# Attention probabilities split into f16 pairs in rows and transposed by DMA, value products one step later, norms summed along rows

## The chip, the cores and the metric

The kernel runs on one core of a Trainium2 chip. The metric is the device time of one execution in microseconds (us). A core has TensorE (PE in the profile; its weight loads are PEld), VectorE (DVE), ScalarE (ACT), GpSimd (POOL) and SyncE (SP). Here SP does no arithmetic: it issues every DMA of the kernel, in one queue, in order.

## The reference, cut to what matters

One layer over 2048 tokens of width 1024, all in float32. Only the parts that the change meets are quoted in full:

```
h = rms_norm(x, g1)                        # mean of x*x over a token's 1024 values
p = h @ W_in                               # q, k, v of 8 heads x 64, conv and pool channels
q = rms_norm(q);  k = rms_norm(k)          # per head
scores = q k^T / 8 + bias(head, distance)  # own 64-token chunk and the 8 chunks before it
probs  = softmax(scores);  y = probs @ v
x = x + concat(y, conv, pool) @ W_out
x = x + square(relu(rms_norm(x, g2) @ W1)) @ W2      # 1024 -> 4096 -> 1024
```

## The kernel before

The work is done in four blocks of 512 tokens (`block`, L385) and then in an MLP stage (L995) that needs all blocks. A float32 product is made from pairs (a high part, and what is left of it), with three matmuls for a product (`mm3`, L159). In the MLP, and for probabilities times values, both parts are f16.

**A block.** `project` (L402) is called three times, for q, k and v. In the first call `load_x` (L390) also loads x transposed (features on partitions), splits it, squares it (ACT, L208) and adds the squares up on POOL (L209); four small TensorE products with a column of ones (`token_cols`, L211, L214) sum this over the features, and `rsqrt` turns it into a factor for each token. Then attention runs, woven with dense work.

**Attention** has 32 units in a block: 4 head pairs x 2 heads x 4 tiles of 128 query rows. A unit has up to 5 tiles of 128 keys (640 columns; in block 0 only 1 to 4 tiles, since nothing lies before it). `scores` (L517) makes the scores on TensorE (L529, L530), adds the bias and takes the row maximum on DVE (L533), and takes the exponential on ACT (L539) into `sb`: 128 queries x up to 640 keys, float32. `flip` (L542) transposes `sb` with TensorE in tiles of 128x128 against the identity (L550), at most 512 columns into one PSUM bank `pt`; ACT makes the f16 high part from PSUM (L551), scaled by `PSC`, and DVE the rest (L552), both into `pp` (two buffers). `values` (L555) multiplies each tile of `pp` by the values, three matmuls of 64 columns for each key tile (L565).

**Order.** `weave` (L75) writes the order of TensorE's instructions by hand: for each step of `attention` (L581) it takes a share of the side work, which is the output projection of the block before, then the conv and pool channels of this one (`side`, L760). Within the step of unit n, TensorE gets the scores of n, side work, the transposes of unit n-1, the value products of unit n-2, and side work. TensorE follows that order strictly. The other engines and SP have an order of their own, fixed when the program is built, with `attention` given the higher priority; each runs it in order.

**Surveys.** The MLP works in f16 with scales taken from the norms of its weights. `survey` (L267) loads all of W1 and W2 once (128 loads of 256 KB, `pr` L281 and `ps` L298) in small steps among the side work. For W1 it squares on ACT (L283), adds three times on POOL (L286 to L288) and sums with TensorE products against ones (L271). For W2 each row's sum comes from ACT's accumulator (L300). In block 3, `early_operands` (L348) prepares the first MLP operands among the conv steps.

**Buffers.** `scr`, `hd` and `p1` lie in SBUF. A tile of a pool with `bufs=n` takes the place of the n-th one before it, and its first writer waits until all readers of that one are done, DMAs included.

Of the kernel before, what the change touches and what calls it, by code (L numbers as in the profile page):

```python
# [18 lines left out]
P = 128  # L19
# [73 lines left out]
def trunk(ctx, tc, xT, cols, cinv, w_qkv, w_cp, w_out, w1, w2, nbias, pool_w, outT):  # L93
# [32 lines left out]
    ones16 = const.tile([P, 1], BF16, name="ones16")  # L126
    ve.memset(ones16, 1.0)
# [75 lines left out]
    def sumsq(acc, src, first, pool):  # L203
        if first:
            sc.activation(acc, src, AF.Square)
        else:
            q = pool.tile([P, TB + 16], F32, tag="win", bufs=2, name="sq")[:, :TB] if pool is scr else pool.tile([P, 512], F32, tag="sq", bufs=1, name="sq")
            sc.activation(q, src, AF.Square)  # L208
            gp.tensor_tensor(out=acc, in0=acc, in1=q, op=ALU.add)  # L209
# [16 lines left out]
    vacc = p1.tile([P, 512], F32, name="vacc")  # L226
# [11 lines left out]
    def value_norms(k):  # L238
        raw = scr.tile([P, 512], F32, tag="x", bufs=5, name=f"vw{k}")
# [18 lines left out]
    cn = const.tile([P, FF // P], F32, name="cn")  # L258
# [8 lines left out]
    def survey():  # L267
        def norms(f0, group):
            t = pd(f"cn{f0}")
            for i in range(8):  # L270
                te.matmul(t[:, i : i + 1], group[:, i], ones16, start=True, stop=True)  # L271
            ve.tensor_copy(cn[:, f0 : f0 + 8], t[:, 0:8])

        full = None
        for ft in range(FF // P):
            if ft % 8 == 0:
                group = scr.tile([P, 8, P], BF16, tag="pg", bufs=2, name=f"pg{ft}")
            qs = []
            for half in range(2):
                raw = scr.tile([P, 512], F32, tag="x", bufs=5, name=f"pr{ft}_{half}")  # L280
                sy.dma_start(raw, w1[ft, half])  # L281
                q = scr.tile([P, 4, P], BF16, tag="pq", bufs=3, name=f"pq{ft}_{half}")
                paced(sc.activation(q.rearrange("p a b -> p (a b)"), raw, AF.Square))  # L283
                qs.append(q)
            q = qs[0]
            gp.tensor_tensor(out=q, in0=q, in1=qs[1], op=ALU.add)  # L286
            gp.tensor_tensor(out=q[:, :2], in0=q[:, :2], in1=q[:, 2:], op=ALU.add)
            gp.tensor_tensor(out=group[:, ft % 8], in0=q[:, 0], in1=q[:, 1], op=ALU.add)  # L288
            if ft % 8 == 2 and full:
                norms(*full)  # L290
            if ft % 8 == 7:
                full = (ft - 7, group)
            yield
        yield
        norms(*full)
        for i in range(64):
            raw = scr.tile([P, 512], F32, tag="x", bufs=5, name=f"ps{i}")
            sy.dma_start(raw, w2[i // 16, (i // 2) % 8, i % 2])  # L298
            q = scr.tile([P, 512], BF16, tag="pq", bufs=3, name=f"pt{i}")
            paced(sc.activation(q, raw, AF.Square, accum_out=sq2[:, i : i + 1]))  # L300
            if i % 2:
                yield

# [21 lines left out]
    def scales():  # L325
        for _ in surveyed:
            pass
        m = const.tile([P, 4], F32, name="m")
        ve.tensor_reduce(out=m[:, 0:1], in_=cn, axis=AX.X, op=ALU.max)
# [12 lines left out]
        ve.tensor_scalar(m[:, 3:4], m[:, 3:4], 2.0**-17, None, op0=ALU.mult)  # L342
        ve.tensor_tensor(out=beta, in0=m[:, 3:4], in1=p[:, 1:2], op=ALU.mult)
# [4 lines left out]
    def early_operands():  # L348
        for k in range(4):
            q = {}  # L350
            for n in range(2):
                rr = scr.tile([P, 512], F32, tag="x", bufs=5, name=f"er{k}_{n}")
                sy.dma_start(rr, r2d[n])
                for half in range(2):
                    kk = k + 4 * half
                    t = scr.tile([P, 512], F32, tag="x", bufs=5, name=f"e{k}_{half}{n}")
                    sy.dma_start(t, x2d[kk, :, n * 512 : n * 512 + 512])
                    ve.scalar_tensor_tensor(out=t, in0=t, scalar=g2s[:, kk : kk + 1], in1=rr, op0=ALU.mult, op1=ALU.mult)
# [26 lines left out]
    def block(b, prev_out):  # L385
        t0 = b * TB
        xgs = [p1.tile([P, 2, TB], F32R, tag="xg", bufs=KT, name=f"xg{b}_{k}") for k in range(KT)]
        acc = p1.tile([P, TB], F32, tag="acc", name=f"acc{b}")

        def load_x(k):  # L390
            xr = scr.tile([P, 512], F32, tag="x", bufs=5, name=f"x{b}_{k}")
            sy.dma_start(xr, xT[k * P : (k + 1) * P, t0 : t0 + TB])
            g = col[:, C_G1 + k : C_G1 + k + 1]
            xg = xgs[k]
            sc.activation(xg[:, 0], xr, AF.Copy, scale=g)
            ve.scalar_tensor_tensor(out=xg[:, 1], in0=xr, scalar=g, in1=xg[:, 0].bitcast(F32), op0=ALU.mult, op1=ALU.subtract)
            sumsq(acc, xr, k == 0, scr)
# [4 lines left out]
        def project(c, also=lambda k: None):  # L402
# [3 lines left out]
            else:  # L406
                ac = [pd(f"a{b}_{c}_{i}", "dydt"[i]) for i in range(4)]
            for k in range(KT):
                if c == 0:
                    load_x(k)  # L410
                w = load_w(w_qkv[c, k], f"wq{b}_{c}_{k}", 1)
# [4 lines left out]
                also(k)  # L416
            return ac

        acq = project(0)
        ms1 = token_cols(acc, f"ms1_{b}")  # L420
        rstd = rsqrt(sm, ms1, NT, "r1")
        epsq = sm.tile([P, NT], F32, tag="epsq", name=f"epsq{b}")
        ve.tensor_scalar(epsq, ms1, EPS, None, op0=ALU.mult)
# [80 lines left out]
        ve.tensor_scalar(vr, rstd, vsc[:, 0:1], None, op0=ALU.mult)  # L504
# [7 lines left out]
        rb = row_bcast(rstd, f"rb{b}")  # L512
# [29 lines left out]
        def flip(u, st, sb, lo_t, nk, vp):  # L542
            hp, j, i = u
            h = 2 * hp + j
            pp = hd.tile([P, 2, 640], F16, tag="pp", name=f"pp{b}_{h}_{i}")
            for c0, c1 in ((0, nk),) if nk <= 512 else ((0, 384), (384, nk)):
                pt = pd(f"pt{b}_{h}_{i}_{c0}", "t")
                n = c1 - c0
                for m in range(n // P):
                    te.transpose(pt[:, m * P : (m + 1) * P], sb[:, c0 + m * P : c0 + (m + 1) * P], ident)  # L550
                sc.activation(pp[:, 0, c0:c1], pt[:, :n], AF.Copy, scale=PSC)  # L551
                ve.scalar_tensor_tensor(out=pp[:, 1, c0:c1], in0=pt[:, :n], scalar=PSC, in1=pp[:, 0, c0:c1], op0=ALU.mult, op1=ALU.subtract)  # L552
            return u, st, pp, lo_t, nk // P, vp

        def values(u, st, pp, lo_t, nkt, vp):  # L555
# [525 lines left out]
```

## Time and profile before

| what | value |
|---|---|
| median of 3 runs | 2143.21 us (2143.02 to 2146.45) |
| the profiled execution | 2144.97 us; span of its instructions 2143.1 us |
| mean granted TensorE clock | 0.986 of full speed |
| busy: PE, DVE, ACT, POOL | 96%, 64%, 47%, 33% of the span |
| DMA | 58% of the span of 16 engines, 392.88 MB |
| attention of blocks 0 to 3, first score matmul to last | about 86 to 164, 252 to 402, 489 to 637, 743 to 885 us |
| MLP stage | from about 970 us to the end |

Time outside the span is 1.9 us. "Busy" of an engine is the union of its instructions' spans. "Idle before" names what ended a wait, by the semaphores. DMA share is the mean busy share of the 16 DMA engines. "Landing" is the time from a DMA's issue to its completion.

### The profile page before, as it was taken

The numbers are of one execution on the slowest core, as the hardware profiler recorded it, in microseconds if no ns is written. First come the engines' busy times: TensorE is split into PE (matmuls) and PEld (weight loads), VectorE is DVE, ScalarE is ACT, GpSimd is POOL, SyncE is SP. The second block draws the span as 40 slices with busy tenths as digits, with TensorE's granted clock in tenths as the row PEclk, the third lists the DMA queues.
The fourth block names the chain that finished last, engine by engine and source line by source line (L and its number), as shares of the span: only waits on it lengthen the run. The fifth ranks groups of instructions, "written<-read, shape, count | busy, mean of one in ns | idle before, by whom it ended". The sixth has DMA issues, their size and how long they took to land.

```text
span 2143.1 us, 31845 instructions
## 1 busy us (share of the span) xinstructions
PE 2050.1 (96%) x11136; PEld 1262.3 (59%) x11136; DVE 1365.9 (64%) x2184; ACT 1010.9 (47%) x1940; POOL 700.1 (33%) x565
## 2 busy tenths in 40 slices
PE   7999998999899699998999999999999999999999
PEld 6777787888787588864444444444444444444444
DVE  7687466856679767757768878767743053353354
ACT  5466465737665455545656446446134151150330
POOL 4254055200224213154546456445522031130132
PEclk9999999999999899999999999999999999999999
DMA  8685698549866776493465565547743333333344
GB/s 287 202 242 169 173 273 248 179 121 273 266 199 211 241 225 179 136 344 116 161 221 189 174 209 182 182 148 286 259 120 102 104 101 101 103 97 106 103 148 152
DMA packets 215824, 392.88 MB, mean 183 GB/s; under 512 B 25584, under 2 KB 32880, under 8 KB 215664
## 3 DMA queue, kind: packets, MB, share of 16 engines
q1 hardware_dynamic: 215664, 390.86, 58.2%
q8 instruction: 87, 1.43, 0.3%
q14 instruction: 73, 0.60, 0.1%
HBM read 268.60 MB, written 105.38 MB: 175 GB/s over the span
## 4 chain that ended last, share of the span: by engine, by line
PE 68%; DMA 10%; DVE 9%; issue 5%; POOL 4%; ACT 3%; SPq 1%; POOLq 0%; DVEq 0%; ACTq 0%
PE b_d L845 21%; PE b_u L845 18%; PE a L161 3%; PE a L162 3%; PE a L160 3%; PE cp L160 2%; PE o L160 2%; PE cp L161 2%; PE cp L162 2%; PE o L161 2%; PE o L162 2%; PE pt L550 2%; PE y L565 2%; DMA r_d<-w 1%; PE s L529 1%
## 5 line engine op out<-in xcount | busy, mean ns | idle before, releaser
L845 PE MATMUL b_d<-ft_u,s_d 128*128 128x512 f16 x1152 | 265.8, 381 | 7.6 <-ACT ft_u L795 3.2
L845 PEld LDWEIGHTS <-s_d 128*128 128x128 f16 x1536 | 150.5, 98 | 191.3 <-issue 10.6
L845 PEld LDWEIGHTS <-s_u 128*128 128x128 f16 x1536 | 150.6, 98 | 186.5 <-issue 7.2
L845 PE MATMUL b_u<-zt,s_u 128*128 128x512 f16 x1152 | 257.3, 381 | 1.5 <-DVE u2u L948 0.8
L966 DVE TENSOR_TENSOR acc<-acc,b_d 128x512 f32<-128x512 f32 x176 | 119.1, 682 | 179.7 <-PE b_d L845 175.4
L845 PEld LDWEIGHTS <-a_u 128*128 128x128 f16 x1152 | 112.8, 98 | 146.6 <-issue 13.5
L845 PEld LDWEIGHTS <-a_d 128*128 128x128 f16 x1152 | 112.8, 98 | 143.2 <-issue 8.4
L829 POOL TENSOR_TENSOR t1u<-u2u,c11u 128x512 f32<-128x512 f32 x32 | 43.6, 1363 | 443.5 <-ACT u2u L952 431.3
L845 PE MATMUL b_d<-fb_u,a_d 128*128 128x512 f16 x768 | 183.7, 379 | 4.0 <-DVE acc L966 1.7
L845 PE MATMUL b_u<-zb,a_u 128*128 128x512 f16 x768 | 176.6, 379 | 1.3 <-ACT u2u L935 1.3
L209 POOL TENSOR_TENSOR acc<-acc,sq 128x512 f32<-128x512 f32 x56 | 82.8, 1479 | 260.4 <-ACT sq L208 191.3
L161 PE MATMUL a<-wq,xg 128*128 128x512 f32 x384 | 155.3, 404 | 8.2 <-DVE wq L142 8.2
L160 PE MATMUL a<-wq,xg 128*128 128x512 f32 x384 | 147.4, 407 | 10.4 <-ACT wq L141 7.8
L162 PE MATMUL a<-wq,xg 128*128 128x512 f32 x384 | 154.5, 403 | 0.1
L539 ACT ACTIVATE sb<-sb,nm 128x640 f32<-128x640 f32 (+4 forms) x128 | 97.6, 762 | 115.8 <-DVE nm L533 111.5
L552 DVE SCALAR_TENSOR_TENSOR pp<-pt,pp 128x384 f16<-128x384 f32 (+1 forms) x224 | 101.8, 483 | 48.2 <-ACT pp L551 47.6
L533 DVE CUSTOM_DVE_ANT_0 sb<-s,b 128x640 f32<-128x640 f32 (+4 forms) x128 | 94.1, 735 | 52.7 <-PE s L530 51.3
L142 DVE TENSOR_TENSOR wq<-rwq,wq 128x512 fp32r<-128x512 f32 x96 | 79.9, 839 | 46.0 <-ACT wq L141 46.0
L160 PE MATMUL o<-mix,wo 128*128 128x512 f32 x256 | 106.3, 416 | 1.3 <-ACT mix L631 1.0
L160 PE MATMUL cp<-xg,wc 128*128 128x512 f32 x256 | 107.1, 418 | 0.0
L141 POOL CAST wc<-rwc 128x512 fp32r<-128x512 f32 x64 | 41.8, 653 | 195.4 <-PE cp L162 94.2
L935 ACT COPY u2u<-b_u 128x512 f32<-128x512 f32 x32 | 18.5, 578 | 179.8 <-PE b_u L845 177.5
(274 smaller groups left out, 4512.1 us busy)
## 6 DMA issues: line engine op xcount, KB each, us to landing
rwq<-w_qkv SPq DMA_DIRECT2D x96, 256.0 KB, 2.8
pr<-w SPq DMA_DIRECT2D x64, 256.0 KB, 4.8
rwc<-w_cp SPq DMA_DIRECT2D x64, 256.0 KB, 4.3
rwo<-w_out SPq DMA_DIRECT2D x64, 256.0 KB, 4.4
ps<-w SPq DMA_DIRECT2D x64, 256.0 KB, 4.5
r_u<-w SPq DMA_DIRECT2D x64, 256.0 KB, 3.4
wd<-s_u SPq DMA_DIRECT2D x64, 256.0 KB, 2.2
r_d<-w SPq DMA_DIRECT2D x64, 256.0 KB, 2.9
```

What stands on the lines that cost most here:

```text
L142: (lo or ve).tensor_tensor(out=w[:, 1], in0=raw, in1=w[:, 0].bitcast(F32), op=ALU.subtract)
L160: te.matmul(out, ah, bh, start=start, stop=False)
L161: te.matmul(out, ah, bl, start=False, stop=False)
L162: te.matmul(out, al, bh, start=False, stop=stop)
L209: gp.tensor_tensor(out=acc, in0=acc, in1=q, op=ALU.add)
L533: ve.tensor_tensor_reduce(out=sb[:, :nk].rearrange("p (e k) -> p e k", e=ne), in0=s[:, :ne, :hk], in1=bi[:, 640 - nk :].rearrange("p (e k) ...
L539: exps.append(sc.activation(sb[:, :nk], sb[:, :nk], AF.Exp, bias=nmx, scale=-1.0, accum_out=st["l"][:, i, j : j + 1]))
L550: te.transpose(pt[:, m * P : (m + 1) * P], sb[:, c0 + m * P : c0 + (m + 1) * P], ident)
L552: ve.scalar_tensor_tensor(out=pp[:, 1, c0:c1], in0=pt[:, :n], scalar=PSC, in1=pp[:, 0, c0:c1], op0=ALU.mult, op1=ALU.subtract)
L829: gp.tensor_tensor(out=t1, in0=b12, in1=b11, op=ALU.subtract)
L845: te.matmul(bank, w[:, a, q * P : (q + 1) * P], xs[q][:, c], start=start and q == 0 and i == 0, stop=q == n - 1 and i == 2, skip_group_che ...
L966: ve.tensor_tensor(out=a, in0=a, in1=bk, op=ALU.add)
```

## The change

The scores stay as they are. `flip` no longer uses TensorE: ACT makes the f16 high part directly from `sb` in rows, DVE the rest, both into a new tile `ph` with **one** buffer, and SP issues two DMA transposes (one for each part) from `ph` to `pp`, which now has three buffers. The value products of a unit come one step later (unit n-3 in the step of unit n). Token norms of x come from a second copy of x in rows (`xN`, 32 more loads of 256 KB), squared and summed by ACT's accumulator; W1's norms in the same way from a transposed copy (`w1t`), as W2's already were. With it go the POOL sums of these norms and their TensorE products. `early_operands` loads `r2d` twice instead of eight times and loads a step ahead. Several scratch pools get other sizes.

```diff
 def survey():
+    srcs = [w1t[i // 2, i % 2] for i in range(64)] + [w2[i // 16, (i // 2) % 8, i % 2] for i in range(64)]
+    held = []
+    def look():
+        i, raw = held.pop(0)
+        acc = (sq1, sq2)[i // 64][:, i % 64 : i % 64 + 1]
+        paced(sc.activation(raw, raw, AF.Square, accum_out=acc))
+    for i, src in enumerate(srcs):
+        raw = scr.tile([P, 512], F32, tag="sv", bufs=4, name=f"{'prt'[2 * (i // 64)]}{i}")
+        sy.dma_start(raw, src)
+        held.append((i, raw))
+        if i % 2:
+            while len(held) > 2:
+                look()
+            yield
...
 def load_x(k):
-    xr = scr.tile([P, 512], F32, tag="x", bufs=5, name=f"x{b}_{k}")
+    xr = scr.tile([P, 512], F32, tag="sv", bufs=4, name=f"x{b}_{k}")
...
-    sumsq(acc, xr, k == 0, scr)
+def row_power(n):
+    raw = scr.tile([P, 512], F32, tag="sv", bufs=4, name=f"xn{b}_{n}")
+    sy.dma_start(raw, xN[4 * b + n // 2, n % 2])
+    return n, raw
+def look_rows(n, raw):
+    sc.activation(raw, raw, AF.Square, accum_out=sx[:, n // 2, n % 2 : n % 2 + 1])
...
-ms1 = token_cols(acc, f"ms1_{b}")
+    ve.tensor_reduce(out=ms1, in_=sx, axis=AX.X, op=ALU.add)
+    ve.tensor_scalar(ms1, ms1, 1.0 / D, EPS, op0=ALU.mult, op1=ALU.add)
...
 def flip(u, st, sb, lo_t, nk, vp):
-    pp = hd.tile([P, 2, 640], F16, tag="pp", name=f"pp{b}_{h}_{i}")
-    for c0, c1 in ((0, nk),) if nk <= 512 else ((0, 384), (384, nk)):
-        pt = pd(f"pt{b}_{h}_{i}_{c0}", "t")
-        n = c1 - c0
-        for m in range(n // P):
-            te.transpose(pt[:, m * P : (m + 1) * P], sb[:, c0 + m * P : c0 + (m + 1) * P], ident)
-        sc.activation(pp[:, 0, c0:c1], pt[:, :n], AF.Copy, scale=PSC)
-        ve.scalar_tensor_tensor(out=pp[:, 1, c0:c1], in0=pt[:, :n], scalar=PSC, in1=pp[:, 0, c0:c1], op0=ALU.mult, op1=ALU.subtract)
+    ph = hd.tile([P, 2, 640], F16, tag="ph", bufs=1, name=f"ph{b}_{h}_{i}")
+    sc.activation(ph[:, 0, :nk], sb[:, :nk], AF.Copy, scale=PSC)
+    ve.scalar_tensor_tensor(out=ph[:, 1, :nk], in0=sb[:, :nk], scalar=PSC, in1=ph[:, 0, :nk], op0=ALU.mult, op1=ALU.subtract)
+    pp = hd.tile([P, 2, 5, P], F16, tag="pp", bufs=3, name=f"pp{b}_{h}_{i}")
+    for part in range(2):
+        sy.dma_start_transpose(pp[:, part, : nk // P], ph[:, part, :nk])
...
 def attention(first):
-    for u in units + [None, None]:
+    for u in units + [None, None, None]:
...
-        flipping = flip(*scored) if scored else None
-        if flipped:
-            done = values(*flipped) or done
-        flipped, scored = flipping, got
+        if scored:
+            flipped.append(flip(*scored))
+        if flipped and (u is None or len(flipped) > 2):
+            done = values(*flipped.pop(0)) or done
+        scored = got
```

## Rows read from the trace of the kernel before

**Rows 1.** The page, part 1: busy us, share of the span, instructions.
```profile
PE 2050.1 (96%) x11136; PEld 1262.3 (59%) x11136; DVE 1365.9 (64%) x2184; ACT 1010.9 (47%) x1940; POOL 700.1 (33%) x565
```

**Rows 2.** Engines by stage: attention of blocks 0 to 3, MLP; last: clock, DMA share, GB/s.
```profile
86.00:164.00 78.00, 72.10 (x551) 60.08 (x550) 61.80 (x152) 51.37 (x127) 41.09 (x51) 0.98 0.86 253
252.00:402.00 150.00, 142.69 (x1138) 123.03 (x1139) 99.45 (x208) 94.63 (x215) 67.83 (x80) 0.97 0.82 243
489.00:637.00 148.00, 140.90 (x1115) 121.54 (x1116) 98.99 (x202) 99.38 (x253) 27.41 (x29) 0.98 0.83 251
743.00:885.00 142.00, 141.28 (x1120) 122.78 (x1121) 98.90 (x205) 75.17 (x166) 27.10 (x29) 0.98 0.60 171
970.00:2143.00 1173.00, 1142.22 (x5252) 514.99 (x5252) 685.05 (x846) 465.12 (x778) 414.17 (x282) 1.00 0.48 153
```

**Rows 3.** Timeline of PE in block 1, one unit: start us, us.
```profile
304.50 0.71 PE L550 MATMUL pt<-ident,sb 128*128 128x128 f32 x5
305.05 0.42 PE L565 MATMUL y<-vp,pp 128*128 128x64 f16 x9
...
308.91 0.71 PE L550 MATMUL pt<-ident,sb 128*128 128x128 f32 x5
309.45 0.34 PE L565 MATMUL y<-vp,pp 128*128 128x64 f16 x6
```

**Rows 4.** Instruction groups: ACT and DVE splits, from PSUM (pt) and from SBUF.
```profile
L551 ACT ACTIVATE pp<-pt 128x384 f16<-128x384 f32 (+1 forms) x224 | 86.7, 427 | 23.7 <-PE pt L550 23.3 <-ACT pp L551 0.2
L552 DVE SCALAR_TENSOR_TENSOR pp<-pt,pp 128x384 f16<-128x384 f32 (+1 forms) x224 | 101.8, 483 | 48.2 <-ACT pp L551 47.6
L364 ACT CAST et<-e 128x512 f16<-128x512 f32 x16 | 9.9, 617 | 27.1 <-DMA xd<-eb 15.5 <-DMA xd<-et 8.7 <-DVE wq L142 1.7
L365 DVE TENSOR_TENSOR et<-e,et 128x512 f16<-128x512 f32 x16 | 12.1, 758 | 7.5 <-ACT et L364 7.5
L799 DVE SCALAR_TENSOR_TENSOR a_d<-r_d,sw,a_d 128x512 f16<-128x512 f32 x48 | 54.0, 1130 | 0.9 <-ACT a_d L798 0.9
```

**Rows 5.** DMA issues in attention of blocks 0, 1, 2, 3 in turn: KB each, median us to landing.
```profile
kd<-khi SPq DMA_DIRECT2D x6, 128.0 KB, 2.4
qs<-qhi SPq DMA_DIRECT2D x6, 128.0 KB, 4.3
...
kd<-khi SPq DMA_DIRECT2D x6, 128.0 KB, 4.4
qs<-qhi SPq DMA_DIRECT2D x6, 128.0 KB, 6.6
...
kd<-khi SPq DMA_DIRECT2D x6, 128.0 KB, 4.5
qs<-qhi SPq DMA_DIRECT2D x6, 128.0 KB, 6.9
...
kd<-khi SPq DMA_DIRECT2D x6, 128.0 KB, 2.6
qs<-qhi SPq DMA_DIRECT2D x6, 128.0 KB, 5.0
```

**Rows 6.** Line L475 (qs and qx, SBUF to SBUF), the whole span.
```profile
DMA to landing us min/median/max: 2.2/5.4/8.4
```

**Rows 7.** Line L281 on SP's queue: ns that an issue holds it, min/median/max.
```profile
L281 SPq DMA_DIRECT2D pr<-w x64: 327/382/2107, 31.2 to 347.9; - x64
```

**Rows 8.** Instruction groups of the norms: TensorE sums, POOL sums, ACT accumulator.
```profile
L214 PE MATMUL ms<-ones,acc 128*128 128x1 f32 x64 | 8.0, 239 | 0.0
L286 POOL TENSOR_TENSOR pq<-pq,pq 128x512 bf16<-128x512 bf16 x32 | 38.5, 1204 | 119.4 <-ACT pq L283 119.3
L300 ACT ACTIVATION_READ_ACCUMULATOR pt<-ps 128x1 f32 x64 | 12.1, 188 | 0.0
```

**Rows 9.** Engines in the first projection of block 0, columns as in rows 2.
```profile
8.00:31.00 23.00, 19.84 (x75) 15.56 (x75) 19.62 (x27) 15.28 (x26) 13.86 (x10) 0.93 0.89 298
```

**Rows 10.** Waits of PE, whole span: us in total, times, longest.
```profile
PE s L529 <- DMA qx<-qlo: 13.0, 1, 13.0
...
PE pt L550 <- DVE pp L552: 5.8, 3, 3.5
```

More of the change, by code (lines that the diff above doesn't have):

```diff
@@ L92, in trunk @@
 @with_exitstack
-def trunk(ctx, tc, xT, cols, cinv, w_qkv, w_cp, w_out, w1, w2, nbias, pool_w, outT):
+def trunk(ctx, tc, xT, xN, cols, cinv, w_qkv, w_cp, w_out, w1, w1t, w2, nbias, pool_w, outT):
     nc = tc.nc
@@ L125, in trunk @@
     ve.memset(ones, 1.0)
-    ones16 = const.tile([P, 1], BF16, name="ones16")
-    ve.memset(ones16, 1.0)
     qgs = const.tile([P, 1], F32, name="qgs")
@@ L206, in sumsq @@
         else:
-            q = pool.tile([P, TB + 16], F32, tag="win", bufs=2, name="sq")[:, :TB] if pool is scr else pool.tile([P, 512], F32, tag="sq", bufs=1, name="sq")
+            q = pool.tile([P, 512], F32, tag="sq", bufs=1, name="sq")
             sc.activation(q, src, AF.Square)
@@ L225, in trunk @@
     vsc = const.tile([P, 2], F32, name="vsc")
-    vacc = p1.tile([P, 512], F32, name="vacc")
+    vacc = p1.tile([P, 512], F32, tag="acc", name="vacc")
     def power_above(p):
@@ L238, in value_norms @@
     def value_norms(k):
-        raw = scr.tile([P, 512], F32, tag="x", bufs=5, name=f"vw{k}")
+        raw = scr.tile([P, 512], F32, tag="x", bufs=2, name=f"vw{k}")
         sy.dma_start(raw, w_qkv[2, k])
@@ L256, in value_scale @@
         ve.tensor_scalar(vsc[:, 1:2], r, 1.0 / (1024.0 * PSC), None, op0=ALU.mult)
-    cn = const.tile([P, FF // P], F32, name="cn")
+    sq1 = const.tile([P, 64], F32, name="sq1")
     sq2 = const.tile([P, 64], F32, name="sq2")
@@ L267, in survey @@
     def survey():
[L268 to L300, printed above, removed]
+        srcs = [w1t[i // 2, i % 2] for i in range(64)] + [w2[i // 16, (i // 2) % 8, i % 2] for i in range(64)]
[8 more added lines that the diff above has]
+            held.append((i, raw))
             if i % 2:
+                while len(held) > 2:
+                    look()
                 yield
+        while held:
+            look()
     surveyed = survey()
@@ L328, in scales @@
         m = const.tile([P, 4], F32, name="m")
+        cn = sm.tile([P, FF // P], F32, tag="ss", name="cn")
+        ve.tensor_reduce(out=cn, in_=sq1.rearrange("p (f t) -> p f t", t=2), axis=AX.X, op=ALU.add)
         ve.tensor_reduce(out=m[:, 0:1], in_=cn, axis=AX.X, op=ALU.max)
@@ L348, in early_operands @@
     def early_operands():
-        for k in range(4):
[L350 to L358, printed above, removed]
+        rr = []
+        for n in range(2):
+            t = scr.tile([P, 512], F32, tag="x", bufs=2, name=f"er{n}")
+            sy.dma_start(t, r2d[n])
+            rr.append(t)
+        for k in range(4):
+            raw, q = {}, {}
+            for half in range(2):
+                for n in range(2):
+                    raw[half, n] = scr.tile([P, 512], F32, tag="sv", bufs=4, name=f"e{k}_{half}{n}")
+                    sy.dma_start(raw[half, n], x2d[k + 4 * half, :, n * 512 : n * 512 + 512])
+            yield
+            for half in range(2):
+                for n in range(2):
+                    kk, t = k + 4 * half, raw[half, n]
+                    ve.scalar_tensor_tensor(out=t, in0=t, scalar=g2s[:, kk : kk + 1], in1=rr[n], op0=ALU.mult, op1=ALU.mult)
                     q[half, n] = t
-                    yield
+                yield
             def put(src, op):
-                t = scr.tile([P, 2, 512], F16, tag="pg", bufs=2, name=f"e{op}_{k}")
+                t = scr.tile([P, 2, 512], F16, tag="pg", bufs=1, name=f"e{op}_{k}")
                 sc.copy(t[:, 0], src)
@@ L387, in block @@
         xgs = [p1.tile([P, 2, TB], F32R, tag="xg", bufs=KT, name=f"xg{b}_{k}") for k in range(KT)]
-        acc = p1.tile([P, TB], F32, tag="acc", name=f"acc{b}")
         def load_x(k):
-            xr = scr.tile([P, 512], F32, tag="x", bufs=5, name=f"x{b}_{k}")
+            xr = scr.tile([P, 512], F32, tag="sv", bufs=4, name=f"x{b}_{k}")
             sy.dma_start(xr, xT[k * P : (k + 1) * P, t0 : t0 + TB])
@@ L396, in load_x @@
             ve.scalar_tensor_tensor(out=xg[:, 1], in0=xr, scalar=g, in1=xg[:, 0].bitcast(F32), op0=ALU.mult, op1=ALU.subtract)
-            sumsq(acc, xr, k == 0, scr)
+        sx = sm.tile([P, NT, 2], F32, tag="sx", name=f"sx{b}")
+        def row_power(n):
[4 more added lines that the diff above has]
+            sc.activation(raw, raw, AF.Square, accum_out=sx[:, n // 2, n % 2 : n % 2 + 1])
         nrm = {}
@@ L407, in project @@
                 ac = [pd(f"a{b}_{c}_{i}", "dydt"[i]) for i in range(4)]
+            rows = []
             for k in range(KT):
@@ L410, in project @@
                     load_x(k)
+                if c == 0:
+                    rows.append(row_power(k))
+                    if k:
+                        look_rows(*rows.pop(0))
                 w = load_w(w_qkv[c, k], f"wq{b}_{c}_{k}", 1)
@@ L416, in project, with row_stats @@
                 also(k)
+            for r in rows:
+                look_rows(*r)
             return ac
         acq = project(0)
-        ms1 = token_cols(acc, f"ms1_{b}")
-        rstd = rsqrt(sm, ms1, NT, "r1")
-        epsq = sm.tile([P, NT], F32, tag="epsq", name=f"epsq{b}")
-        ve.tensor_scalar(epsq, ms1, EPS, None, op0=ALU.mult)
+        rstd, epsq = [], sm.tile([P, NT], F32, tag="epsq", name=f"epsq{b}")
+        def row_stats():
+            ms1 = sm.tile([P, NT], F32, tag="ms", name=f"ms1_{b}")
+            ve.tensor_reduce(out=ms1, in_=sx, axis=AX.X, op=ALU.add)
+            ve.tensor_scalar(ms1, ms1, 1.0 / D, EPS, op0=ALU.mult, op1=ALU.add)
+            ve.tensor_scalar(epsq, ms1, EPS, None, op0=ALU.mult)
+            rstd.append(rsqrt(sm, ms1, NT, "r1"))
+        row_stats()
         def normalize(ac, nm):
@@ L503, in block @@
         vr = sm.tile([P, NT], F32, tag="vr", name=f"vr{b}")
-        ve.tensor_scalar(vr, rstd, vsc[:, 0:1], None, op0=ALU.mult)
+        ve.tensor_scalar(vr, rstd[0], vsc[:, 0:1], None, op0=ALU.mult)
         for i in range(NT):
@@ L511, in block @@
                 sy.dma_start(vd[b % 2, h], v[:, h].rearrange("p t s d -> p (t s d)"))
-        rb = row_bcast(rstd, f"rb{b}")
+        rb = row_bcast(rstd[0], f"rb{b}")
         sc.copy(R, rb)
@@ L562, in values @@
                 vv = vp[:, a] if a < 4 else v[:, h, a - 4]
-                ms_ = slice(m * P, (m + 1) * P)
                 for r, (pi, vi) in enumerate(((0, 0), (0, 1), (1, 0))):
-                    te.matmul(st["y"][:, i, j], pp[:, pi, ms_], vv[:, vi], start=(m == 0 and r == 0), stop=(m == nkt - 1 and r == 2))
+                    te.matmul(st["y"][:, i, j], pp[:, pi, m], vv[:, vi], start=(m == 0 and r == 0), stop=(m == nkt - 1 and r == 2))
             if j == 1 and i == NT - 1:
@@ L583, in attention @@
             yield LEAD if b else LEAD * RATE / RATE0
-            scored = flipped = done = None
+            scored = done = None
+            flipped = []
             units = [(hp, j, i) for hp in range(H // 2) for j in range(2) for i in range(NT)]
-            for u in units + [None, None]:
+            for u in units + [None, None, None]:
                 if u:
@@ L1062 @@
     arrays = {
+        "xN": np.ascontiguousarray(a["x"][0].reshape(16, 128, 2, 512).transpose(0, 2, 1, 3)),
         "xT": np.ascontiguousarray(a["x"][0].T),
@@ L1069 @@
         "w1": w1,
+        "w1t": np.ascontiguousarray(a["w_mlp1"][0].T.reshape(32, 128, 2, 512).transpose(0, 2, 1, 3)),
         "w2": w2,
```

## The prediction

> **What bounds the kernel now.** I read the page first: TensorE is busy for 96% of the span, no other engine above 64% [rows 1]. So only two things can change the time much: work taken from TensorE, or a wait put in front of it. Then the engines by stage, because the change lives in the four attention stages (518 us together) and leaves the 1173 us of the MLP alone [rows 2]. In the attention of blocks 1 to 3 TensorE is busy for 143 of 150, 141 of 148 and 141 of 142 us, ACT for 63%, 67% and 53%, DVE for 66% to 70%, and the DMA engines for 82%, 83% and 60%. Then the timeline of one unit: five transposes start at 304.50, the value products behind them at 305.05, and the next unit's transposes at 308.91 [rows 3]. A unit is thus 4.41 us long (32 of them make 141 us), of which the transposes hold TensorE for 0.55 us. In block 0 a unit is 78 / 32 = 2.44 us. TensorE hardly waits for the split there: 5.8 us in the whole span [rows 10].
>
> **What is removed.** Block 0 has 80 transposes (8 rounds of 1, 2, 3 and 4 tiles), blocks 1 to 3 have 96 units of 5: 560 at 0.11 us each are 62 us, all on the path. This is the whole prize; it is 2.9%. Half of the 64 token sums at 239 ns, 4 us, go too [rows 8]. The POOL sums (the largest is 38.5 us) were beside TensorE on an engine that is 33% busy, so I cost their removal at nothing. The 96 accumulator reads added on ACT, 188 ns each, make 18 us; ACT's 40% of free time covers them, and without that cover they would cost at most these 18 us.
>
> **What is added, per unit.** ACT makes the high part in one instruction: 617 ns for 512 columns from SBUF, so 0.77 us for 640. DVE makes the rest: 758 ns for 512 columns, so 0.95 us, at worst 1130 ns, 1.41 us, as in the MLP; I take 0.95, since the row is from block 3's own stage [rows 4]. In block 0, with 320 columns on average, the two are 0.86 us. In sum this is about what the splits from PSUM took (two of 427 and two of 483 ns), so neither engine becomes the bound. Then come two DMAs of up to 160 KB and their landing, T.
>
> **The new loop.** `ph` has one buffer. ACT's split of the next unit may begin only when both transposes of this unit have read it. So a unit cannot be shorter than ACT + DVE + T, whatever TensorE does; three `pp` buffers and the later value products hide the length of this chain, but not its rate. TensorE would now need 4.41 - 0.55 = 3.86 us. With 1.72 us of ACT and DVE, the full gain needs T of at most 2.1 us, and T above 2.7 us makes a unit longer than before. Behind the waiting split on ACT stand the next exponential and the weight splits; behind a transpose that waits for DVE on SP's queue stand the weight loads. The one who waits last is TensorE, at the value products.
>
> **T.** The trace has no transpose by DMA. The nearest row from below is `kd<-khi`: issued in twos behind an ACT and a DVE split, 128 KB, landing in 2.4, 4.4, 4.5 and 2.6 us in blocks 0 to 3. From above it is `qs<-qhi`, SBUF to SBUF, but in fours behind larger loads: 4.3, 6.6, 6.9 and 5.0 us [rows 5]. The shortest of any SBUF to SBUF copy was 2.2 us, the longest 8.4 [rows 6]. I take a third of the way from `kd` to `qs`, as the pattern is that of `kd` and the two ends of the transfer those of `qs`: 3.0, 5.1, 5.3 and 3.4 us.
>
> Two pages of the Trainium skill pull apart here. "Advanced Engine Details and Errata", section "X-Bar Transpose (TRN2)", says that such transposes run as fast as regular DMAs; by it the `kd` end holds, and the sum would be near +119. "VectorE: DVE Perf Modes", section "The three transpose paths", gives 1309 ns by DMA against 390 ns by TensorE for one 128x128 tile; five in a row would be an estimated 6.5 us for a part, near `qs`, and the sum near +404. Its 390 ns isn't what this trace has, where a tile costs 0.11 us [rows 3].
>
> **The sum.** Blocks 0 to 3: loops of 3.86, 6.82, 7.02 and 5.12 us, times 32: 124, 218, 225 and 164 us against 78, 150, 148 and 142, so +46, +68, +77 and +22 = +213. Token sums -4. The second copy of x adds 2 MB to the first projection, where DMA is 89% busy at 298 GB/s [rows 9]: 2 MB at 335 GB/s is 6 us, between 0 and +6; I take +4. In later blocks these loads lie in projections, in which nothing waits for them. Fewer `r2d` loads may end or move the one wait of 13.0 us before block 3's scores [rows 10]: -13 to +13, taken as 0. The extra step at each block's end lies beside side work of the next stage: 0, at most one unit, 4.4 us, for each block. Total +213 on the profiled execution of 2145.0: 2358. The median of the runs is 1.8 us lower, so I say 2356.
>
> With T at `kd` the same sum is +119 (2262), at `qs` +404 (2547). In the long loop TensorE would idle for 3 of 6.8 us. Its granted clock is 0.97 to 0.98 in these stages and 1.00 in the MLP [rows 2]; if it fell to the 1.2 GHz level, 3.86 us of work would be 7.7 us, and blocks 1 and 2 would each gain some 0.8 us x 32 = 26 us more. That lies within the upper end.
>
> **Rivals.**
>
> *The gain arrives.* T is about that shortest copy, 2.2 us, since a transpose stays inside SBUF. The loop is then 3.92 us in blocks 1 to 3 (-25, -23, -17) and 3.06 in block 0 (+20): 2099. For it: in this range the loop and TensorE's need nearly coincide, and a loop that slows the kernel also lightens the DMA engines. Against it: medians from 2.4 to 6.9 us while DMA is 60% to 86% busy. It decides where T is under 2.7 us. The bottom, with nothing but the 62 us gone, is 2083.
>
> *SP becomes the bound.* An issue holds SP's queue for 382 ns in the middle and 2107 at most [rows 7]; a transpose, with many small pieces, may be like the longest. Block 1 moves 243 GB/s x 150 us = 36 MB, some 140 issues of 256 KB, 53 us; 64 transposes of 2.1 us add 135: 188 us (+38). Blocks 2, 3 and 0 (half as long transposes) in the same way give +41, +28 and +18: 2270.
>
> *The DMA engines become the bound.* Blocks 1 and 2 need 123 us of them each now [rows 2]; 10.5 MB of transposes at 296 GB/s add 35: 158 us each. Block 0 comes to 85, block 3 is TensorE's 124. Sum +7: 2152. At half that rate for small pieces it is +130, 2275. Against: it presumes that every other latency is hidden.
>
> *Long transposes.* T is the 8.4 us of the longest copy: loops of 10.1 us, 9.3 in block 0, +750: 2895. Against: that copy stood behind others.
>
> **How the numbers follow.** The loop at a T of `kd` to `qs`: 0.47, own range 2260 to 2550. The gain arrives: 0.24. SP: 0.12. DMA engines: 0.10, of which 0.04 is no change. Long transposes: 0.07. A change within 0.2% (4 us) is about what a measurement of this kernel can't tell from none. So faster 0.25, same 0.04, slower 0.71. From 2085, which takes in the gain nearly whole, to 2520, which leaves out the long transposes and the top of the forecast, 0.8 is held. The likeliest is 2356.
>
> **What would show it.** Step by step: L550 and `pt` are gone, and TensorE loses some 62 us of busy time; the spacing of the exponentials in block 1 is 6 to 7 us and not 4.4; ACT's split into `ph` waits for the DMA of `pp`, about half the unit; TensorE's waits stand at the value products, released by the transposes; the transposes land in 3 to 5.5 us; the MLP keeps its 1173 us. I am wrong if the transposes land within 2.7 us, or if the unit in blocks 1 to 3 is 3.9 us; and wrong in mechanism, though not in sign, if ACT's split doesn't wait for `pp` while SP's queue or the DMA share is full.

## The result, and the profile after

The changed kernel takes 2359.53 us (median of 4 runs, 2356.42 to 2361.3) against 2143.11 us: a ratio of 1.101, 95% interval 1.099 to 1.103. It is slower by 216 us; forecast were 2356 us and +213.

First the engines by stage of the changed kernel, the attention of blocks 0 to 3 and then the MLP (columns as in [rows 2]):

```profile
84.00:237.00 153.00, 93.94 (x493) 68.09 (x492) 64.68 (x159) 57.74 (x155) 14.29 (x18) 0.74 0.61 162
329.00:528.00 199.00, 145.73 (x984) 113.35 (x982) 102.11 (x179) 102.77 (x227) 29.26 (x29) 0.88 0.94 234
620.00:819.00 199.00, 145.09 (x982) 113.20 (x981) 102.03 (x179) 104.30 (x231) 28.74 (x29) 0.88 0.94 236
917.00:1098.00 181.00, 144.35 (x987) 112.17 (x987) 119.63 (x196) 82.10 (x149) 42.11 (x37) 0.92 0.89 207
1123.00:2357.00 1234.00, 1206.72 (x5538) 556.42 (x5536) 716.77 (x886) 489.13 (x818) 438.10 (x299) 0.99 0.49 161
```

The stretches here run from the first exponential of a block to the last, those of [rows 2] by the score matmuls. Taken by the exponentials in both kernels, the four stages are 154, 200, 201 and 182 us long and not 84, 152, 149 and 140: +71, +49, +51 and +43, together +213. All that lies before, between and after them takes 1620 us in place of 1619.

TensorE's granted clock fell to 0.74 in block 0, 0.88 in blocks 1 and 2 and 0.92 in block 3. That is one reason why its busy time did not fall though the transposes are gone: a 512-column `cp` product took 431 ns in block 1 on average, and 405 before. Another is that the longer stage holds more of the side work (184 `cp` products and not 164). The DMA engines, at 0.82 in block 1 before, are busy for 0.94 of a longer stage.

Then, on the page, the groups that the change made:

```profile
L557 DVE SCALAR_TENSOR_TENSOR ph<-sb,ph 128x640 f16<-128x640 f32 (+4 forms) x128 | 102.5, 801 | 223.1 <-ACT ph L556 222.6
...
L556 ACT ACTIVATE ph<-sb 128x640 f16<-128x640 f32 (+4 forms) x128 | 85.5, 668 | 161.7 <-DMA pp<-ph 152.8
```

and the waits of the whole span (engine, line, releaser: us in total, times, longest):

```profile
ACT ph L556 <- DMA pp<-ph: 152.8, 95, 4.4
...
PE y L572 <- DMA pp<-ph: 83.1, 68, 7.2
PE s L539 <- DVE nm L543: 69.0, 59, 4.1
PE o L158 <- ACT wo L139: 44.6, 4, 12.1
PE cp L158 <- POOL wc L139: 14.3, 2, 13.8
```

ACT's split stood idle 153 us, in 95 of 128 units, until a transpose had read `ph`. TensorE waits for the transposes at the value products (83 us), for score banks that DVE has not yet emptied (69 us; DVE itself stood idle 223 us for ACT's split, in its row above), and six times for a weight (45 + 14 us).

The transposes on SP's queue (line L560: ns that an issue holds it, min/median/max; then us to landing):

```profile
L560 SPq DMA_TRANSPOSE pp<-ph x256: 1127/1214/2554, 85.7 to 1107.0; - x128
...
DMA to landing us min/median/max: 2.3/3.2/6.8
```

and their median landing in the attention of blocks 0, 1, 2 and 3 in turn, among the DMA issues:

```profile
pp<-ph SPq DMA_TRANSPOSE x60, 2.5
...
pp<-ph SPq DMA_TRANSPOSE x60, 3.7
...
pp<-ph SPq DMA_TRANSPOSE x60, 3.5
...
pp<-ph SPq DMA_TRANSPOSE x60, 3.2
```

And one turn of the loop in the timeline of block 1 (start us, us):

```profile
442.22 0.82 DVE L557 SCALAR_TENSOR_TENSOR ph<-sb,ph 128x640 f16<-128x640 f32 x1
...
443.07 1.48 SPq L560 DMA_TRANSPOSE pp<-ph  x1
...
448.31 0.73 ACT L556 ACTIVATE ph<-sb 128x640 f16<-128x640 f32 x1
...
449.08 1.20 DVE L557 SCALAR_TENSOR_TENSOR ph<-sb,ph 128x640 f16<-128x640 f32 x1
...
449.42 2.66 SPq L560 DMA_TRANSPOSE pp<-ph  x2
```

DVE ends at 443.04, the second transpose is issued at 443.07, and ACT writes the next `ph` only at 448.31. Averaged over the 31 turns of block 1, the records of the trace give for the links of the loop: ACT 0.73 us, to DVE's start 0.24, DVE 0.87, to the second part's issue 0.94, from there to its landing 3.59, to ACT's next start 0.36. Together that is 6.7 us. In 106 of 124 turns of the four blocks ACT's split starts within 0.3 us of the landing. So the loop is closed nearly everywhere: the next split follows the landing at once.

### The profile page after: what moved, and what is told of

Its sections match the earlier page's. It is cut to its first block, busy times and chain, and to the rows that moved or that the text cites. A ratio compares the mean times of both kernels' runs of the same rounds, so it can differ in the third digit from the quotient of the medians.

```text
span 2357.8 us, 30751 instructions
## 1 busy us (share of the span) xinstructions
PE 2070.1 (88%) x10512; PEld 1223.7 (52%) x10512; DVE 1340.4 (57%) x2088; ACT 1028.9 (44%) x1940; POOL 582.1 (25%) x441
## 5 line engine op out<-in xcount | busy, mean ns | idle before, releaser
L557 DVE SCALAR_TENSOR_TENSOR ph<-sb,ph 128x640 f16<-128x640 f32 (+4 forms) x128 | 102.5, 801 | 223.1 <-ACT ph L556 222.6
L539 PE MATMUL s<-kx,qs 128*128 128x320 f32 (+1 forms) x224 | 81.6, 370 | 84.9 <-DVE nm L543 69.0
L556 ACT ACTIVATE ph<-sb 128x640 f16<-128x640 f32 (+4 forms) x128 | 85.5, 668 | 161.7 <-DMA pp<-ph 152.8
L207 POOL TENSOR_TENSOR acc<-acc,sq 128x512 f32<-128x512 f32 x28 | 36.9, 1319 | 476.9 <-ACT sq L206 476.8
L158 PE MATMUL cp<-xg,wc 128*128 128x512 f32 x256 | 119.1, 465 | 21.9 <-POOL wc L139 14.3
L572 PEld LDWEIGHTS <-pp 128*128 128x128 f16 x1680 | 66.0, 103 | 133.6 <-DMA pp<-ph 105.8
```

Of the source, the lines that this page charges most:

```text
L158: te.matmul(out, ah, bh, start=start, stop=False)
L539: te.matmul(s[:, e, :hk], qs[:, i * P : (i + 1) * P], kx[:, ks], start=True, stop=False)
L556: sc.activation(ph[:, 0, :nk], sb[:, :nk], AF.Copy, scale=PSC)
L557: ve.scalar_tensor_tensor(out=ph[:, 1, :nk], in0=sb[:, :nk], scalar=PSC, in1=ph[:, 0, :nk], op0=ALU.mult, op1=ALU.subtract)
L572: te.matmul(st["y"][:, i, j], pp[:, pi, m], vv[:, vi], start=(m == 0 and r == 0), stop=(m == nkt - 1 and r == 2))
```

## The experiments

Ratios are to runs of the kernel before on the same chip. Differences in us are between medians, in part of different chips, on which the kernel before took 2141 to 2146 us. "In the middle" is a median.

### The norms alone

The flip, `values` and `attention` of before, with all the rest of the change.

```diff
-    ph = hd.tile([P, 2, 640], F16, tag="ph", bufs=1, name=f"ph{b}_{h}_{i}")
...
+    pp = hd.tile([P, 2, 640], F16, tag="pp", name=f"pp{b}_{h}_{i}")
...
+            te.transpose(pt[:, m * P : (m + 1) * P], sb[:, c0 + m * P : c0 + (m + 1) * P], ident)
```

> The norms, the surveys and the buffer sizes of the change, with the flip, the value products and the step of before (TensorE transposes). My theory, that all of the loss comes from the one ph buffer, has this at the time before within 8 us: 2135 to 2151 (4 us of token sums gone from TensorE, 4 us more for the second copy of x, the POOL sums hidden). A rival, that the second copy of x and the accumulator reads on ACT cost a part of the 216 us: above 2160.

2142.06 us, ratio 0.9993 (0.9976 to 1.0009), as expected. The norms, the surveys and the buffer sizes leave the time as it was. The whole loss lies in the flip by DMA, together with the later value products that go with it.

They do move time from one stretch to another, though. Attention in blocks 0 to 3 of `e1`, by the exponentials:

```profile
84.00:166.00 82.00, 74.64 (x575) 63.02 (x575) 63.44 (x161) 54.98 (x156) 13.95 (x18) 1.00 0.84 247
249.00:398.00 149.00, 142.47 (x1118) 122.68 (x1117) 100.19 (x204) 99.15 (x254) 27.02 (x29) 0.97 0.80 246
483.00:632.00 149.00, 141.40 (x1121) 121.83 (x1120) 98.96 (x204) 100.21 (x257) 26.38 (x29) 0.98 0.81 248
726.00:880.00 154.00, 142.50 (x1120) 121.73 (x1119) 111.84 (x222) 79.80 (x176) 39.51 (x37) 0.99 0.62 180
```

Block 3 takes 154 us here, with TensorE as busy as before (142.5 and 141.3 us), and the stretch ahead of it is shorter by about as much (94 us; 106 in [rows 2]). So a later run is best laid beside `e1`, block by block. For the changed kernel this gives +71, +50, +50 and +27 us in the stages, and some 22 us more outside them.

### Two ph buffers, with a control

For the space, scratch `s` has two tiles and some small statistics tiles one; `e2` has that alone, `e3` the second `ph` as well.

```diff
-    ph = hd.tile([P, 2, 640], F16, tag="ph", bufs=1, name=f"ph{b}_{h}_{i}")
+    ph = hd.tile([P, 2, 640], F16, tag="ph", bufs=2, name=f"ph{b}_{h}_{i}")
```

> Control for the next run: the changed kernel with 2.5 KB per partition taken from other buffers (three scratch tiles become two, small statistics tiles one). Within 1% of the changed kernel's 2359.5 us if these buffers don't matter; if conv and pool wait for scratch, above 2385.

2364.34 us, ratio 1.102 (1.099 to 1.105), as the changed kernel (1.101): the smaller buffers don't matter.

> As e2, but ph has two buffers, so ACT's split of a unit no longer waits for the transposes of the unit just before. If the loop through the one buffer is all that costs time: half the loop is 3.4 us, TensorE (3.86 us a unit) or SP (two issues of 1.2 us and the rest, about 4.5 us a unit) bound again, 2100 to 2200 us. If the DMA engines stand right behind it (they were busy for 0.94 of 199 us in the attention of blocks 1 and 2, so 187 us of work there, 161 in block 3 and 93 in block 0): about 2270 us, and a DMA share near 1. If the loop is not the cause: as e2.

2329.67 us, ratio 1.086 (1.083 to 1.089). Only 35 us came back, beside `e2`. That fits none of the three theories: it is more than the loop alone leaves (2100 to 2200), more than the 2270 named for the DMA engines, and less than `e2`. The profile of `e3` tells more. Its stages in blocks 0 to 3:

```profile
87.00:229.00 142.00, 84.49 (x490) 64.58 (x490) 61.46 (x156) 56.60 (x154) 14.76 (x18) 0.76 0.63 168
319.00:513.00 194.00, 137.69 (x985) 112.18 (x984) 97.18 (x177) 101.62 (x225) 27.91 (x29) 0.85 0.95 239
602.00:793.00 191.00, 137.69 (x985) 112.26 (x984) 98.44 (x179) 102.27 (x228) 27.44 (x29) 0.84 0.96 243
890.00:1076.00 186.00, 141.07 (x986) 112.48 (x985) 117.87 (x195) 81.10 (x146) 40.52 (x37) 0.88 0.87 201
```

and its waits of TensorE and of ACT's split:

```profile
PE o L158 <- ACT wo L139: 56.0, 4, 14.5
PE cp L158 <- POOL wc L139: 50.0, 5, 18.9
PE y L572 <- DMA pp<-ph: 48.1, 34, 5.3
...
ACT ph L556 <- DMA pp<-ph: 84.8, 40, 5.4
```

TensorE's waits for transposes fell from 83 to 48 us, and its waits for weights rose from 59 us (6 times) to 106 us (9 times). ACT still waits for a free `ph`, but for 85 us in 40 units and not 153 in 95. In the other units its splits run ahead, and the transposes queue on SP: a first part is issued 2.0 to 2.8 us after ACT's end, in the changed kernel 0.2 to 0.5 (averages by block). Behind them in the order stand the weight loads. Two candidates for what binds now are SP's queue and the DMA engines, at 0.95 in blocks 1 and 2.

### One transpose for both parts

```diff
...
-    for part in range(2):
-        sy.dma_start_transpose(pp[:, part, : nk // P], ph[:, part, :nk])
+    sy.dma_start_transpose(pp[:, : 2 * nk // P], ph[:, : 2 * nk])
...
```

> One DMA transpose for both parts of a unit (up to 10 tiles) in place of two: 128 issues and not 256, the same bytes, still one ph buffer. By the loop: ACT 0.73, DVE with its waits 1.1, then one issue to landing of some 4 to 4.5 us, 6 to 6.5 us against 6.7: 2310 to 2365 us. If SP's issue time of 1.2 us were the bound: 128 issues of 1.2 us less, 154 us: about 2205 us.

2350.42 us, ratio 1.096 (1.093 to 1.100). Halving the issues with one `ph` gives only 9 us, within the range of the loop. SP's issue time is not what bounds the changed kernel. In block 1 the wait from DVE's end to the issue fell from 0.94 to 0.20 us, but the one landing takes 4.46 us where the second part's took 3.59, and a turn is no shorter (6.9 us).

> e3 (two ph buffers, 2329.7 us) and e4 (one DMA transpose for both parts) together. What holds e3 back? Theory SP: its queue issues for 155 of the 194 us of attention in block 1 (81 for transposes, 74 for the rest), the transposes start 2 to 3 us late there and the weight loads stand behind them. One issue of 1.5 us in place of two of 1.2 takes some 30 us from SP in each block: 2210 to 2240 us. Theory DMA engines: they are 95% busy in blocks 1 and 2, and the bytes stay: above 2300 us.

2246.21 us, ratio 1.049 (1.047 to 1.051), 6 us above the range named for SP and far below that for the DMA engines. With two `ph` the same edit gives 83 us. An issue holds SP's queue for 1.45 us in the middle, in place of two of 1.2 (line L559, as above):

```profile
L559 SPq DMA_TRANSPOSE pp<-ph x128: 1167/1446/3777, 89.7 to 991.9; - x128
...
DMA to landing us min/median/max: 2.5/4.2/6.9
```

So in `e3` the issues on SP's queue held it back: the bytes are the same, and the DMA engines' work nearly so, 178 us in block 1 (0.98 x 182) and 184 in `e3` (0.95 x 194). The queue itself was not full there, with issues for 155 of the 194 us; this points to its order, in which transposes and loads stand behind each other. The gain is uneven: the stages of blocks 0 to 3 are 27, 12, 16 and 28 us shorter, least where the DMA engines were near full in `e3`. In `e5` they are full in blocks 1 to 3 (0.98, 1.03, 1.00; a packet counts in the stretch in which it starts, so a share can pass 1):

```profile
288.00:470.00 182.00, 131.89 (x973) 106.90 (x972) 99.91 (x179) 102.84 (x225) 28.94 (x29) 0.88 0.98 253
561.00:736.00 175.00, 134.80 (x977) 109.32 (x977) 98.71 (x178) 103.20 (x228) 29.44 (x29) 0.88 1.03 263
831.00:989.00 158.00, 135.54 (x981) 109.34 (x981) 117.69 (x193) 81.25 (x147) 42.80 (x37) 0.92 1.00 239
```

### The loads from POOL's queue

```diff
 def load_w(src, name, shape, hi=None, lo=None):
-    sy.dma_start(raw, src)
+    gp.dma_start(raw, src)
...
 def survey():
-        sy.dma_start(raw, src)
+        gp.dma_start(raw, src)
```

> e3, with the weight loads of the blocks (224) and the survey loads (128) issued from POOL's queue, no longer from SP's; the same bytes on the same DMA engines. Theory SP: SP loses some 30 to 40 us of issues in each of blocks 1 to 3 and no load stands behind a transpose: 2150 to 2230 us. Theory DMA engines: 2310 to 2340 us, or more if POOL's way of issuing is slower.

2342.6 us, ratio 1.093 (1.090 to 1.096), in what was named for the DMA engines.

> Two ph buffers, one transpose for both parts, and the loads from POOL's queue. Theory SP: TensorE bounds attention again, 2090 to 2160 us. Theory DMA engines: above 2280 us.

2309.98 us, ratio 1.078 (1.074 to 1.081), as named for the DMA engines. Both are slower than the same kernel with all DMAs from SP (by 13 and 64 us). The transposes of `e7` are no longer behind loads on their queue, but they land later: 5.2 us in the middle and 19.2 at most, against 4.2 and 6.9 in `e5`:

```profile
DMA to landing us min/median/max: 2.3/5.2/19.2
```

The DMA engines were full here too, and the same bytes cost them more time. In block 1 of `e7` they worked 191 us (1.01 x 189) for 45 MB, in `e5` 178 us for 46 MB:

```profile
293.00:482.00 189.00, 137.54 (x954) 109.78 (x952) 97.86 (x176) 98.94 (x223) 66.41 (x101) 0.89 1.01 238
```

So taking the loads off SP's queue does not help while the engines are full. Why the transposes land later beside loads of a second queue is not shown. As a test of SP alone the edit is not clean: an issue of a load takes 536 ns of POOL, among POOL's other work, where it held SP for 330 to 380 in the middle.

### The load of the DMA engines

The survey is left out, from `e5` (`e8`) and from the changed kernel (`e12`).

```diff
 def survey():
-    srcs = [w1t[i // 2, i % 2] for i in range(64)] + [w2[i // 16, (i // 2) % 8, i % 2] for i in range(64)]
...
+    ve.memset(sq1, 0.6)
+    ve.memset(sq2, 0.16)
+    for i in range(64):
+        yield
```

> e5 (two ph buffers, one transpose for both parts, 2246.2 us) with the survey left out: the 128 loads of W1 and W2 for the norms and their squares are not made, and constants stand for the sums. In e5 the DMA engines are busy for 0.98, 1.03 and 1.00 of the attention of blocks 1 to 3. Theory DMA engines: 33.5 MB less, some 0.85 us of them a load, takes about 20, 37 and 37 us from blocks 0 to 2 and nothing from block 3: 2140 to 2170 us, and the long waits for weights go in blocks 1 and 2. Theory in-order queue (weights stand behind transposes on SP, whatever the load): above 2215 us.

2167.48 us, ratio 1.011 (1.009 to 1.013): 79 us less, the forecast of the DMA engines. Blocks 1 and 2 are back at 149 and 148 us and block 3, which has no survey, stays at 157 (blocks 0 to 3):

```profile
87.00:193.00 106.00, 76.09 (x496) 59.01 (x495) 68.62 (x162) 47.13 (x117) 15.04 (x18) 0.87 0.74 184
276.00:425.00 149.00, 129.71 (x962) 104.93 (x961) 101.33 (x180) 75.43 (x135) 29.27 (x29) 0.94 0.97 233
508.00:656.00 148.00, 129.75 (x958) 104.93 (x957) 99.72 (x179) 74.77 (x135) 28.43 (x29) 0.94 0.99 233
751.00:908.00 157.00, 133.39 (x986) 106.72 (x985) 115.82 (x192) 81.06 (x146) 40.99 (x37) 0.95 0.99 235
```

Beside `e1` (82, 149, 149 and 154 us) nearly all that is left of the loss lies in block 0; what binds there, with the DMA engines at 0.74, is open. In blocks 1 to 3 the engines are still at 0.97 to 0.99: TensorE is busy for only 130 of 149 us in block 1, and the stage is no shorter than with its transposes. The survey's loads also leave SP's queue, so this run alone doesn't part the two. The shares near 1 in `e5`, and `e7`, where loads left SP's queue and the time rose, speak for the DMA engines; a run that eases them alone is not here.

> The changed kernel (one ph buffer, two transposes a unit, 2359.5 us) with the survey left out as in e8. In the loop through ph, ACT, DVE and the two issues stay (about 3 us of the 6.7 in blocks 1 and 2); only the landing can get shorter, from 3.6 to the 2.6 us of block 0. Theory loop: 5.6 to 5.9 us a unit in blocks 1 and 2, some 20 to 30 us less in each, little in blocks 0 and 3: 2295 to 2325 us. Theory DMA engines alone, as between e5 and e8: 80 us or more less, 2280 us or below.

2313.73 us, ratio 1.078 (1.074 to 1.082). Here the same load is worth 46 us, within the range of the loop. The stages stay long though the DMA engines are free for a fifth of the time in block 1 (0.81):

```profile
320.00:500.00 180.00, 146.15 (x995) 113.79 (x994) 104.07 (x183) 77.06 (x139) 29.48 (x29) 0.92 0.81 192
```

A turn is 6.1 us in block 1 and 5.0 in block 0. This run shows that in the changed kernel the one `ph` binds and not the DMA engines' load; the load acts through the links of the loop. In block 1 the turn is 0.65 us shorter than in the changed kernel: 0.35 of it is the landing (3.24 us), the rest the waits for the issue and for ACT's next start.

### Copies in place of transposes

```diff
-    sy.dma_start_transpose(pp[:, part, : nk // P], ph[:, part, :nk])
+    sy.dma_start(pp[:, part, : nk // P].rearrange("p m q -> p (m q)"), ph[:, part, :nk])
```

> e3 (two ph buffers, two DMAs a unit, 2329.7 us) with plain copies of the same bytes from ph to pp in place of the transposes; the probabilities stay in rows, so the transposition itself is left out. If what a transpose costs beyond a copy (an issue of 1.2 us against 0.33 to 0.5, small pieces on the DMA engines) holds e3 back: 2120 to 2190 us. If bytes and latency alone do: above 2280 us.

2194.75 us, ratio 1.023 (1.021 to 1.024), just outside the 2190 us named. So 135 us of the loss of `e3` are what a transpose costs beyond a copy of the same bytes. Two prices show. An issue holds SP for 478 ns against some 1215:

```profile
L560 SPq DMA_DIRECT2D pp<-ph x256: 464/478/1930, 88.1 to 945.1; - x128
```

And in block 1 the DMA engines work 0.95 x 157 = 149 us, 26 us more than before the change (0.82 x 150 = 123, [rows 2]). With transposes, in the changed kernel, they work 0.94 x 199 = 187, 64 us more:

```profile
288.00:445.00 157.00, 130.78 (x959) 104.41 (x958) 99.79 (x178) 101.53 (x226) 29.53 (x29) 0.95 0.95 298
```

Beside that, the packets of `e9` and of the changed kernel, for the same bytes:

```profile
DMA packets 256428, 436.34 MB, mean 199 GB/s; under 512 B 32144, under 2 KB 70160, under 8 KB 256272
DMA packets 371117, 436.37 MB, mean 185 GB/s; under 512 B 177552, under 2 KB 184848, under 8 KB 370960
```

The transposes go in some 145,000 packets under 512 bytes. That this is why they cost the engines more is likely, but no run here separates it.

### Only some units by DMA

The diff is that of `e10`; `e11` has `b == NB - 1 and i % 2` for the condition.

```diff
+    if i == 3:
+        ph = hd.tile([P, 1280], F16, tag="ph", bufs=1, name=f"ph{b}_{h}_{i}")
...
+        return u, st, pp, lo_t, nk // P, vp
     for c0, c1 in ((0, nk),) if nk <= 512 else ((0, 384), (384, nk)):
```

> The changed kernel's norms and later value products; of the units only every fourth (i = 3) goes by DMA, with one transpose for both parts and one ph buffer, the others by TensorE as before. The loop through ph is then four units long (17 us) and can't bind. TensorE loses 16 us of transposes (140 of 560 at 0.11 us, and 4 more in block 0). Theory DMA engines: each such unit costs them about 2.2 us, 18 us in each of blocks 1 to 3, which lifts their share from 0.82 to 0.95 in blocks 1 and 2: between 2125 (all gained) and 2160 us (given back in late weights).

2157.62 us, ratio 1.004 (1.0025 to 1.006). ACT's split no longer waits for a transpose, and still the 16 us of TensorE do not show: the run is 11 us slower than before. Attention in blocks 0 and 1, and TensorE's longest wait in the whole span:

```profile
84.00:173.00 89.00, 75.63 (x529) 60.94 (x528) 61.63 (x156) 54.38 (x154) 15.10 (x18) 0.94 0.91 247
261.00:412.00 151.00, 140.92 (x1073) 119.29 (x1072) 99.63 (x201) 99.68 (x248) 26.99 (x29) 0.96 0.91 259
...
PE y L581 <- DMA pp<-ph: 23.7, 13, 4.9
```

Beside `e1` the four stages are 7, 2, 2 and 1 us longer, so most of the loss lies in block 0. The value products wait 23.7 us for transposes, 8.8 of them in block 0. In blocks 1 and 2 the DMA engines are at 0.91 and 0.92 (0.80 and 0.81 in `e1`; 0.95 was forecast). That their load takes the gain there is not shown.

> As e10, but only every second unit of block 3 goes by DMA, where the DMA engines were busy for 0.60 of attention. TensorE loses 9 us there (80 transposes). Theory DMA engines: 85 us of work and 35 more fit into 133 us: 2130 to 2140 us. If the order on SP's queue is what delays weights: 2145 us or more.

2138.27 us, ratio 0.9963 (0.995 to 0.9976): the one version that is faster than both kernels, by 0.4%. Attention in its block 3 is 148 us long, with the DMA share at 0.83:

```profile
740.00:888.00 148.00, 136.97 (x1031) 114.67 (x1030) 112.38 (x207) 79.84 (x162) 42.35 (x37) 0.95 0.83 222
```

Against the 142 us before this looks like a loss. But `e1`, with the same norms, takes 154 us there, so the stage is 6 us shorter. TensorE's busy time there is 5.5 us less; 9 was forecast. That this is the gain from the transposes fits but is not shown: the intervals of `e1` and `e11` meet at 0.9976, and they differ in the later value products too, which were not run alone.

## Why the prediction was right, point by point

- **What bounds, and the prize.** Right. The norms by themselves are worth nothing measurable (`e1`), as costed. The MLP stayed as it was: after the last exponential the kernel takes 1259 us, and 1256 before.
- **The mechanism.** Right for the changed kernel: the loop through one `ph` is closed in 106 of 124 turns, a lighter DMA load shortens it by 0.65 us in block 1 and does not end it (`e12`), and half the issues do not end it either (`e4`). But the loop is not all that stands in the way: a second `ph` gives back 35 us of 220 (`e3` beside `e2`).
- **The terms of the loop.** That 2356 us met 2359.5 so closely is luck: errors in the terms cancel. T was taken as 3.0, 5.1, 5.3 and 3.4 us. The second part lands in 2.6, 3.6, 3.5 and 3.2 us on average, near `kd<-khi` of the same stages (2.4, 4.4, 4.5, 2.6 in [rows 5]), so "a third of the way" was too long. Left out was that the second part can be issued only when the first has left SP's queue (1.2 us): between DVE's end and the issue lie 1.38, 0.94, 0.96 and 0.81 us. Left out, too, were the 0.1 to 0.4 us from ACT to DVE and from the landing to ACT. All this is 1.6 us a turn in block 0, 1.5 in blocks 1 and 2, and 1.1 in block 3. ACT and DVE, at 0.73 and 0.87 in block 1, were sized well. So a turn came out at 6.7 us in block 1, where 6.8 was forecast, and at 5.2 in block 0, where it was 3.9: the issue time doesn't shrink with the tiles.
- **From turns to time.** The forecast for the blocks, +46, +68, +77 and +22, compares with +71, +49, +51 and +43. Block 1 is 19 us under its forecast though its turn was right, since some 30 turns and not 32 fill the stretch of the exponentials; the last ones run on behind it. What lies behind the blocks was put at 0 (the extra step); beside `e1` some 22 us more lie outside the stages. Against the kernel before this can't be seen, as the norms alone take about as much out of these stretches (1619 us before, 1598 in `e1`, 1620 in the changed kernel) and put most of it into block 3. Its +43 is +27 beside `e1`, near the +22 forecast.
- **The clock.** The fall that stood only in the upper end did come: 0.74 in block 0, 0.88 in blocks 1 and 2, the two levels of 1.2 and 2.4 GHz mixed, with TensorE idle for a fifth (block 3) to two fifths (block 0) of these stages. No run shows what the fall cost; that it cost little is argued, from TensorE's idle time (37 to 59 us in each stage).
- **The signs.** The turn in block 1 (6.7 us), ACT's wait for `pp`, the value products released by the transposes, and the MLP came as named. TensorE's busy time did not fall by 62 us but rose from 2050 to 2070, at the lower clock. ACT's wait is not half the unit: 31 us for the 32 units of block 1, since ACT has other work in between. In block 0 the transposes land in 2.5 us, within the 2.7 that was to show the forecast wrong, and the loop is closed there all the same.
- **The two pages of the Trainium skill.** "Advanced Engine Details and Errata", section "X-Bar Transpose (TRN2)", is borne out for landing (3.0 us in the middle in `e3`, against 3.7 for the plain copies of `e9`) and not for the engines' time: a transpose costs them some 2.5 times what a copy costs (64 against 26 us). The estimate from "VectorE: DVE Perf Modes", section "The three transpose paths", 6.5 us for five tiles, is not borne out: parts of five tiles land in 2.6 us at the least and 3.5 in the middle.
- **The rivals.** "The gain arrives" fell less by T than by the links left out. Without the landing they come to 3.1 us a turn in block 1, so even with a T of 2.2 us a turn would be 5.3 us, above the 4.4 of a unit before. SP and the DMA engines were priced as alternatives to the loop, at 2270 and 2152 to 2275 us. They are limits that stand close behind it: a second `ph` gives 35 us, one issue for two 83 more, the survey's load 79 more; with all three the kernel is still 1.1% slower than before. The issue time was put at 2.1 us and is 1.2; the DMA price per byte was nearer the bad end named (half the rate, 70 us for a block's transposes; measured 64).

## What to carry to other kernels

A path with one buffer between two engines and a DMA has a rate of its own, the sum of its links from the buffer's first write to the landing; compare that sum with the time that the bound engine needs for one turn, before looking at busy shares. When you open such a loop, ask what stands next (the issuing queue, then the DMA engines), since the gain ends there. Before moving work from a bound engine to DMA, see how far the DMA engines are free in that very stage: here they were at 0.82 in block 1, where 0.55 us of TensorE a unit was to be saved for some 2 us of theirs. And lay a run beside one that has all but the edit in question: block 3 read as a loss beside the kernel before and as a gain beside `e1`.

## What the runs showed of the hardware that was not expected

- A DMA transpose holds SP's queue for 1.2 us in the middle (1127 ns at least) whether it has one tile or five (1.18 and 1.22), and for 1.45 us with two to ten (`e5`); a plain copy of the same bytes for 0.48 (`e9`).
- The DMA engines took 64 us more than before for the 10.5 MB of transposes of block 1, and 26 us more for plain copies of them (`e9`). The transposes went in some 145,000 more packets under 512 bytes.
- With the loads issued from a second queue while the engines were full, the transposes on the first landed later: 5.2 us in place of 4.2 in the middle and 19.2 in place of 6.9 at most (`e7` against `e5`).
